# Reordering a hybrid decoder block: preparation, branch loads and the seam before the feed-forward part

## The chip, the cores and the metric

The kernel runs on one core of one Trainium2 chip. What counts is the time of one execution on the device in microseconds (us), the median of several. An execution that is profiled has a time and a span (first to last instruction) of its own.

## The reference: what is computed

One layer of a decoder trunk in float32, 1024 tokens of width 1024:

```python
h = rms_norm(x, norm1_g); proj = h @ w_in                      # 1024 x 6912
p_rwkv, p_sb, q_mem, gate_logits = split(proj)
y_a = rwkv7_branch(p_rwkv, ...)       # 8 heads of 64: token shift, decay, delta-rule recurrence
y_b = stick_breaking_branch(p_sb, q_g, k_g)      # 8 heads of 64, causal, q and k normed
y_m = memory_branch(q_mem, mem, ...)  # 4 heads of 128 over 256 memory tokens
x = x + (sum_b sigmoid(gate_b) * (y_b @ w_branch[b])) @ w_out
h = rms_norm(x, norm2_g) @ w_up                                # 1024 x 5632
acc = causal_conv3(h); gate, val = split(acc)
x = x + (silu(gate) * val) @ w_down
```

## The kernel before

Products that need float32 accuracy are made of three passes of the fast type fp32r: a matrix is split in a rounded high part (ScalarE, ACT: a copy, L80) and a low part (a subtraction on GpSimd, POOL, L81, or on VectorE, DVE), and `mm3` adds hi*hi, hi*lo and lo*hi for two 128x512 halves in PSUM. Eight k steps of this make one 128x1024 tile of a projection: 48 matmuls on TensorE (PE).

The program runs in these stages. `startup` (L171) loads x transposed in eight tiles and three weight tiles, splits them (`xhi`, `xlo`), and makes the squares for the norm. `rwkv_prep` (L307) prepares the recurrence for four pairs of heads: `shift_item` projects k, r and v and passes them to `shifted` (L242), which multiplies by the row norm (L248), makes the shifted copy on ACT (L249) and combines both on DVE (L251); `chain` (L374) makes `bk` (L381) and `ra` (L382 to L384), `gram` (L388) has PE multiply them and DVE mask the result (L398), `decayed` and `turned` make what PE transposes. Then follow stick-breaking attention (`sb_attn`, L814), memory attention (`mem_attn`, L1029, with `mem_q` at L1006), the recurrence by chunks (`inverse`, `stage2`, L477), group norm, and the branch products. `branch` (L1145) loads a stored branch output (`load_y`, L1106, DMA at L1110), splits it (`split_y`, L1101 on ACT, L1102 on DVE) and multiplies it by w_branch.

The projections are *items*: generators that yield after every k step. `weave` runs a stage as the main line and takes items from the list in `run` (L1698) as filler, so that PE has a projection between the steps of a stage; `gate_item` (L733) is such a filler, and its `hook` runs a function after a given k. `close_gates` (L710) does the sigmoids of finished gates. The framework's scheduler fixes the order of each engine when the program is built; instructions that are `pinned` keep the order of the program text among themselves, others may be moved. Every engine then runs its list strictly in order, SyncE (SP) its list of DMA issues too.

After these, `out_proj` (L1200) multiplies by w_out for eight token tiles, and `norm` (L1222) and `spread` (L1238) bring each tile normed and transposed into the operand of the up projection. That projection uses a 2x2 scheme with seven products of half size: `sums` (L1257) makes sums of quarters of the operand, called T1 to T4 beside the quarters 11, 21 and 22, and `split` (L1268) makes the high (L1271, ACT) and low part (L1272) of each. `up_phase` (L1326) runs `step(n, i)` for the products i of pair n; the beginning of this part, where the last tile is normed while the first products run, is called the seam. `weight_sums` and the `prep` functions make the weights' sums and splits (L1351, L1354). `down_phase` is untouched.

The tiles come from pools of a fixed number of buffers: three of tag `w4`, four of `A`, eight of `qk`, seven of `at`. A tile's first writer waits until the readers of the buffer's last tile are done; for a load this wait is in SP's list.

## Time and profile before

| | before |
|---|---|
| median of 3 runs | 1858.47 us (1855.64 to 1860.42) |
| profiled execution: its time | 1856.43 us |
| its span | 1854.7 us |
| PE busy in it | 1796.9 us (97%) |
| DVE, ACT, POOL busy | 1170.1, 866.7, 788.6 us |
| mean granted TensorE clock | 0.991 |
| read from and written to device memory | 179 MB, 80 MB |

A line of waits reads: engine and its line, what it waited for, us in total, times, the longest. A line of the timeline reads: start, duration, engine, line, operation, output and inputs, and in brackets how long the engine stood idle before it and for what. A line of windows reads: the stretch, its length, busy time and count of PE, PE's weight loads, DVE, ACT and POOL, then the granted clock, the DMA share and GB/s. All matmuls are issued by the helpers at L112 and L105, so tiles tell them apart: `mm` banks hold projections, `g` banks everything small.

### The profile page before, as it was taken

Reading aid. Unit: us, or ns where it says so; the run is one execution under the profiler, and the core shown is the slowest. Engines: PE = TensorE matmul, PEld = TensorE weight load, DVE = VectorE, ACT = ScalarE, POOL = GpSimd, SP = SyncE. Lnnn points to the kernel's source line nnn. Section 1 sums busy time; section 2 is a strip of 40 time slices with the busy share of each in tenths; the row PEclk is TensorE's granted clock in tenths of the full one; section 3 lists DMA queues with packets and bytes.
Section 4 is the critical chain, followed back from the end, with each engine's and each line's share of the span. In section 5 each row is a group of like instructions: output and inputs, shape, how many; then the busy total and the mean of one; then the engine's idle time right before and its main releaser. Section 6 shows DMA issues by size and latency. Waiting matters only on the chain. (4 is left out here: it accounts for less than half of the span.)

```text
span 1854.7 us, 27269 instructions
## 1 busy us (share of the span) xinstructions
PE 1796.9 (97%) x10468; PEld 1451.4 (78%) x10468; DVE 1170.1 (63%) x1623; ACT 866.7 (47%) x1553; POOL 788.6 (43%) x447
## 2 busy tenths in 40 slices
PE   8999999999999999998999999979999999999999
PEld 6777778778787887776777878768888888878877
DVE  5657664998887514334333882467776777785595
ACT  5443343565565635533443443454454444444433
POOL 2322343222221452122322541487776767545454
PEclk9999999999999999999999999999999999999999
DMA  4155465111112441568654462323232233395475
GB/s 180 58 170 182 158 201 187 49 43 64 40 52 78 112 128 40 177 237 281 229 171 161 163 235 102 114 68 109 95 124 88 97 114 108 120 326 203 141 247 185
DMA packets 122339, 261.28 MB, mean 141 GB/s; under 512 B 28505, under 2 KB 43097, under 8 KB 122082
## 3 DMA queue, kind: packets, MB, share of 16 engines
q1 hardware_dynamic: 84738, 193.71, 32.2%
q10 hardware_dynamic: 33696, 53.23, 7.9%
q0 software_dynamic: 3776, 12.62, 2.2%
q8 instruction: 82, 1.34, 0.3%
q14 instruction: 47, 0.39, 0.1%
HBM read 178.99 MB, written 80.48 MB: 140 GB/s over the span
## 5 line engine op out<-in xcount | busy, mean ns | idle before, releaser
L81 POOL TENSOR_TENSOR wl<-wr,wh 128x1024 fp32r<-128x1024 f32 x77 | 195.0, 2533 | 479.8 <-ACT wh L80 479.8
L112 PE MATMUL mm<-xhi,wh 128*128 128x512 f32 x784 | 266.0, 420 | 9.1 <-ACT xhi L182 7.4
L112 PE MATMUL mm<-xlo,wh 128*128 128x512 f32 x784 | 247.2, 397 | 0.7 <-DVE xlo L183 0.7
L112 PE MATMUL mm<-xhi,wl 128*128 128x512 f32 x784 | 244.4, 393 | 0.0
L112 PEld LDWEIGHTS mm<-xlo,wh 128*128 128x128 f32 x784 | 149.5, 191 | 35.1 <-DVE xlo L183 1.5
L112 PEld LDWEIGHTS mm<-xhi,wl 128*128 128x128 f32 x784 | 148.9, 190 | 33.8 <-POOL wl L81 0.5
L112 PEld LDWEIGHTS mm<-xhi,wh 128*128 128x128 f32 x784 | 138.5, 192 | 39.8 <-issue 9.1
L80 ACT ACTIVATE wh<-wr 128x1024 fp32r<-128x1024 f32 x77 | 81.5, 1059 | 153.8 <-PE mm L112 89.6
L112 PE MATMUL mm<-dw,da 128*128 128x512 f32 x528 | 121.3, 390 | 1.5 <-DVE da L1593 1.4
L112 PE MATMUL mm<-BT,l 128*128 128x512 f32 x504 | 117.9, 389 | 1.0 <-POOL l L1354 1.0
L112 PEld LDWEIGHTS mm<-dw,da 128*128 128x128 f32 x528 | 98.9, 188 | 23.3 <-DVE da L1593 2.3
L1594 POOL TENSOR_TENSOR dw<-draw,dw 128x512 fp32r<-128x512 f32 x55 | 80.5, 1471 | 84.9 <-ACT dw L1592 82.2
L112 PE MATMUL mm<-BT,wh 128*128 128x512 f32 x352 | 109.8, 393 | 3.2 <-DVE u L1406 3.2
L838 DVE TENSOR_TENSOR_SCAN at<-at,nrt 128x128 f32<-128x128 f32 (+3 forms) x64 | 91.2, 1428 | 32.3 <-ACT at L832 32.2
L112 PEld LDWEIGHTS mm<-BT,l 128*128 128x128 f32 x504 | 94.5, 188 | 21.0 <-POOL l L1354 1.4
L112 PE MATMUL mm<-B,wh 128*128 128x512 f32 x352 | 108.5, 389 | 2.1 <-ACT p L1448 2.1
L1593 DVE TENSOR_TENSOR da<-draw,da 128x512 fp32r<-128x512 f32 x77 | 67.0, 878 | 60.3 <-ACT da L1591 59.7
L112 PE MATMUL g<-dw,da 128*128 128x512 f32 x396 | 92.4, 394 | 2.2 <-ACT dw L1592 1.1
L1354 POOL TENSOR_TENSOR l<-it,l 128x1024 fp32r<-128x1024 f32 x21 | 50.8, 2421 | 94.4 <-ACT l L1351 94.4
L112 PEld LDWEIGHTS g<-dw,da 128*128 128x128 f32 x396 | 75.4, 191 | 18.7 <-ACT dw L1592 1.6
L1591 ACT ACTIVATE da<-draw 128x512 fp32r<-128x512 f32 x77 | 48.3, 629 | 84.3 <-PE mm L112 41.0
L169 POOL TENSOR_TENSOR hf<-rs,half 128x16 f32<-128x16 f32 (+1 forms) x17 | 48.5, 2856 | 86.1 <-DVE rs L168 85.7
(329 smaller groups left out, 3982.2 us busy)
## 6 DMA issues: line engine op xcount, KB each, us to landing
wr<-in_w_in_dram SPq DMA_DIRECT2D x50, 512.0 KB, 3.6
draw<-actd SPq DMA_DIRECT2D x77, 256.0 KB, 3.4
draw<-in_w_down_dram SPq DMA_DIRECT2D x55, 256.0 KB, 4.6
at<-scr SPq DMA_DIRECT2D x24, 512.0 KB, 6.2
wr<-in_w_up_dram SPq DMA_DIRECT2D x22, 512.0 KB, 3.5
actd<-gall ACTq DMA_DIRECT2D x44, 256.0 KB, 3.3
rw<-in_w_up_dram SPq DMA_DIRECT2D x20, 512.0 KB, 3.9
gsd<-w ACTq DMA_DIRECT2D x18, 512.0 KB, 2.7
```

What stands on the lines that cost most here:

```text
L80: self.nc.scalar.activation(hi, raw, AF.Copy)
L81: self.nc.gpsimd.tensor_tensor(lo, raw, hi.bitcast(F32), ALU.subtract)
L112: self.pinned(self.nc.tensor.matmul(*a, **k))
L169: nc.gpsimd.tensor_tensor(out, t[:, :n], self.half[:, :n], ALU.pow)
L838: self.pinned(nc.vector.tensor_tensor_scan(sn[:, :W][:, ::-1], sn[:, :W][:, ::-1], self.nrt[:, 1152 - W :][:, ::-1], 1.0, ALU.mult, ALU.max))
L1354: nc.gpsimd.tensor_tensor(lo, src, hi.bitcast(F32), ALU.subtract)
L1591: self.pinned(nc.scalar.activation(A[:, 0], a, AF.Copy))
L1593: self.pinned(nc.vector.tensor_tensor(A[:, 1], a, A[:, 0].bitcast(F32), ALU.subtract))
L1594: nc.gpsimd.tensor_tensor(Wt[:, 1], w, Wt[:, 0].bitcast(F32), ALU.subtract)
```

## The change

At the start the first weight and x tile come in two halves each, with splits of halves; the squares follow one tile late; the parameters' load stands behind the first half of the weight; and eight bf16 matmuls on a tile of zeros stand in front, into a bank that nobody reads. `shifted` returns its last step as a function, which `shift_item` calls one yield later. `chain` makes `ra` ahead of `bk`. `norm_quarter` yields three times ahead of its scaling, and `close_gates` runs at k = 4. In `mem_kv` the sums for the two halves of the memory norm are two items, and in `mem_q` the split is pinned. Branch loads go into `A` tiles, in whose place the low part is then written, and are split in hooks 3 to 6 of the gate item behind the load. At the seam, `norm` is a generator, the low and high splits are separate functions whose order is written out, p's copy is separate from its product, and the splits of 11 and 21 come at tiles 3 and 4.

```diff
+        halves = [slice(0, 512), slice(512, 1024)]
+        idle = self.t4("ys", BF16, 512)
+        nc.vector.memset(idle, 0.0)
+        pt = self.ps("g")
+        for _ in range(8):
+            nc.tensor.matmul(pt, idle[:, :128], idle, start=True, stop=True)
...
+        def square(k):
             sq = self.t4("qk")
-            nc.scalar.activation(sq, raw, AF.Square)
+            nc.scalar.activation(sq, raws[k], AF.Square)
...
+            parts = halves if k == 0 else [slice(0, 1024)]
+            if k == 0:
+                raww = self.pool_wt.tile([128, 1024], F32, name=self.nm("wr"), tag="wr", bufs=2)
+                ws.append(weights(0))
+                for hs in halves:
+                    nc.sync.dma_start(raww[:, hs], self.I["w_in"][first[0]][:, hs])
+                    if hs.start == 0:
+                        nc.sync.dma_start(self.params, self.I["params"])
+                    nc.sync.dma_start(raw[:, hs], src[:, hs])
+                self.split_raw(raww[:, halves[0]], *[w[:, halves[0]] for w in ws[0]])
+            else:
+                if k < 6 and k % 2 == 0:
+                    raww = self.load_w(self.I["w_in"][first[k // 2]])
+                nc.sync.dma_start(raw, src)
+            for hs in parts:
+                nc.scalar.activation(hi[:, hs], raw[:, hs], AF.Copy, scale=self.par("g1", k))
+                nc.vector.scalar_tensor_tensor(lo[:, hs], raw[:, hs], self.par("g1", k), hi[:, hs].bitcast(F32), ALU.mult, ALU.subtract)
+            if k == 0:
+                self.split_raw(raww[:, halves[1]], *[w[:, halves[1]] for w in ws[0]])
+            elif k < 6 and k % 2 == 0:
+                ws.append(self.split_raw(raww, *weights(k)))
+            if k:
+                square(k - 1)
+        square(7)
...
-        out = self.t4(tag)
-        nc.vector.scalar_tensor_tensor(out, pr, self.omm[:, ti : ti + 1], tmp, ALU.mult, ALU.add)
-        return out
+
+        def rest():
+            out = self.t4(tag)
+            nc.vector.scalar_tensor_tensor(out, pr, self.omm[:, ti : ti + 1], tmp, ALU.mult, ALU.add)
+            return out
+
+        return rest
...
-        out.append(self.shifted(ti, "at", pp))
+        rest = self.shifted(ti, "at", pp)
+        yield
+        out.append(rest())
         self.fresh.append(name)
-        yield
...
             bk4, ra4 = (x.rearrange("p (c u s) -> p c u s", c=8, u=2) for x in (bk, ra))
+            nc.vector.tensor_tensor(ra4[:, :, 0], self.c8(r[:, hs]), self.c8(P[:, hs]), ALU.mult)
+            nc.vector.scalar_tensor_tensor(ra4[:, :, 1, 1:64], self.c8(P[:, hs])[:, :, 0:63], -1.0, self.c8(kk[:, hs])[:, :, 1:64], ALU.mult, ALU.mult)
+            nc.vector.tensor_scalar(ra4[:, :, 1, 0], self.c8(kk[:, hs])[:, :, 0], -math.exp(OFF), None, ALU.mult)
             for x, first in ((b, 1), (kp, 0)):
                 for h2 in range(2):
                     q = slice(h2 * 64, h2 * 64 + 64)
                     nc.vector.tensor_tensor(bk4[q, :, first ^ h2], self.c8(x[q, hs]), self.c8(Q[q, hs]), ALU.mult)
-            nc.vector.tensor_tensor(ra4[:, :, 0], self.c8(r[:, hs]), self.c8(P[:, hs]), ALU.mult)
-            nc.vector.scalar_tensor_tensor(ra4[:, :, 1, 1:64], self.c8(P[:, hs])[:, :, 0:63], -1.0, self.c8(kk[:, hs])[:, :, 1:64], ALU.mult, ALU.mult)
-            nc.vector.tensor_scalar(ra4[:, :, 1, 0], self.c8(kk[:, hs])[:, :, 0], -math.exp(OFF), None, ALU.mult)
             self.spill(p, h, 0, ra, nc.sync)
...
-        for _ in range(2):
+        for _ in range(3):
             yield
         turned(0, bp)
         bp = decayed(1, u1[0])
-        for _ in range(4):
+        for _ in range(3):
             yield
...
         self.rsqrt(rs, vs, 16, 1.0 / 64, 64e-5)
-        yield
+        for _ in range(3):
+            yield
...
-            if k == 2:
+            if k == 4:
...
-                nc.scalar.activation(qhi[:, hs], pp[i], AF.Copy, scale=self.par("memq"))
+                self.pinned(nc.scalar.activation(qhi[:, hs], pp[i], AF.Copy, scale=self.par("memq")))
                 nc.scalar.activation(sq[:, hs], pp[i], AF.Square)
-                nc.vector.scalar_tensor_tensor(qlo[:, hs], pp[i], self.par("memq"), qhi[:, hs].bitcast(F32), ALU.mult, ALU.subtract)
+                self.pinned(nc.vector.scalar_tensor_tensor(qlo[:, hs], pp[i], self.par("memq"), qhi[:, hs].bitcast(F32), ALU.mult, ALU.subtract))
...
-        ys = []
+        hi = self.pool_a.tile([128, 4, 1024], F32R, name=self.nm("yhi"), tag="inst")
+        los = [self.t4("A", F32R) for _ in range(4)]
         for k in range(4):
-            y = self.t4("w4")
-            self.nc.sync.dma_start(y, self.yd[b, k])
-            ys.append(y)
-        return self.split_y(ys)
+            self.nc.sync.dma_start(los[k].bitcast(F32), self.yd[b, k])
+
+        def part(k):
+            y = los[k].bitcast(F32)
+            self.pinned(self.nc.scalar.activation(hi[:, k], y, AF.Copy))
+            self.pinned(self.nc.vector.tensor_tensor(los[k], y, hi[:, k].bitcast(F32), ALU.subtract))
+
+        return [(hi[:, k], los[k]) for k in range(4)], [lambda k=k: part(k) for k in range(4)]
...
-            st["y"] = self.load_y(b)
+            st["y"], parts = self.load_y(b)
+            hooks.update({3 + k: parts[k] for k in range(4)})
...
-            x = self.t4()
+            x = self.t4() if tt < 7 else l4("x7", F32)
             sq = self.t4() if tt < 7 else self.pool_l.tile([128, 1024], F32, name="sq7", tag="sp", bufs=1)
             nc.sync.dma_start(x, self.I["x"][tt * 128 : (tt + 1) * 128, :])
...
+            yield
+            self.pinned(nc.vector.tensor_tensor(rs, ss[:, 0:1], ss[:, 1:2], ALU.add))
             self.rsqrt(rs, rs, 1, 1.0 / D, 1e-6)
+            yield
+            self.pinned(nc.scalar.activation(sq, x, AF.Copy, scale=rs))
...
         def late(tt):
             spread(tt, sqs.pop(tt))
             if tt == 3:
-                for i in (0, 1):
-                    operand(("11", "21")[i], self.pool_l, "l4")
-                    split(("11", "21")[i], [halves(j)[i] for j in range(2)], nc.gpsimd)
+                side(0)
...
+        def evacuate(n):
+            p1 = st[n, "p1"] = self.r4("p1", n=512)
+            ins = nc.scalar.activation(p1, st[n, "A"], AF.Copy)
+            if n < 2:
+                self.pinned(ins)
+
         def step(n, i):
             if i == 1:
                 A = st[n, "A"] = bank()
                 product(n, 1, A, True, True)
-                p1 = st[n, "p1"] = self.r4("p1", n=512)
-                nc.scalar.activation(p1, A, AF.Copy)
+                if n:
+                    evacuate(n)
             elif i == 2:
...
         prep1(1)
-        split("T2", src["T2"], nc.vector, old)
-        split("22", src["22"], nc.gpsimd, old)
+        hi("22", old)
+        hi("T1", old, (0,))
+        hi("T2", old)
+        next(norm)
+        lo("T1", old, (0,))
+        next(norm)
+        hi("T1", old, (1,))
+        lo("T2", old)
+        lo("22", old, eng=nc.gpsimd)
         step(0, 1)
-        step(1, 1)
-        late(7)
-        split("T2", src["T2"], nc.vector, new)
-        split("22", src["22"], nc.gpsimd, new)
+        evacuate(0)
+        next(norm, None)
+        st[1, "A"] = bank()
+        product(1, 1, st[1, "A"], True, True)
+        spread()
+        evacuate(1)
+        sums(384, 512, (0,))
+        hi("T1", new)
+        lo("T1", new, (0,))
+        lo("T1", js=(1,))
+        hi("T2", new)
+        lo("T2", new)
         load(1)
-        prep2(0)
-        parts("T1", nc.vector)
         step(0, 2)
+        hi("T3", old)
         step(1, 2)
         prep3(0)
-        parts("T3", nc.vector)
+        sums(384, 512, (1,))
+        lo("T3", old)
+        hi("T3", new)
+        lo("T3", new)
+        hi("22", new)
+        lo("22", new, eng=nc.gpsimd)
         operand("T4", self.pool_a, "A", bufs=4)
-        split("T4", src["T4"], nc.vector)
+        hi("T4")
+        lo("T4")
+        prep2(0)
         st[0, 3] = hl(self.early[3][:, R], self.pool_l, ("l4", "l4"), 512, True)
-        for i in (6, 5, 7, 4, 3):
-            step(0, i)
-            if i == 5:
-                prep2(1)
-            if i == 4:
-                load(2)
+        step(0, 5)
+        prep2(1)
+        step(0, 6)
+        Bk = bank()
+        product(0, 7, Bk, True, True)
+        v = st[0, "u2"] = u_tile()
+        nc.vector.tensor_tensor(v[:, L2], Bk, st[0, "u1"][:, R2], ALU.add)
+        nc.vector.tensor_tensor(v[:, R2], st[0, "C"], v[:, L2], ALU.add)
+        step(0, 40)
+        step(0, 41)
+        load(2)
+        step(0, 3)
         prep3(1)
         for n in range(1, len(pairs)):
             order = (6, 5, 40, 7, 41, 3) if n == 1 else (1, 5, 6, 2, 7, 4, 3)
...
-            items += [*([self.differ] if p == 0 else []), kp, gate(), *([self.spread_last] if p == 0 else []), kss, qp, gate(hooks), mark(f"sb{p}")]
+            items += [*([self.differ] if p == 0 else []), kp, gate({6: self.spread_last} if p == 0 else {}), kss, qp, gate(hooks), mark(f"sb{p}")]
...
-        ld1, br1 = self.branch(1, True)
-        ld2, br2 = self.branch(2, False)
-        items += [lambda: drain(inv), ld1, gate(), gate(), mark("y1"), *br1, ld2, gate(), *br2, gate()]
+        ld1, hk1, br1 = self.branch(1, True)
+        ld2, hk2, br2 = self.branch(2, False)
+        items += [lambda: drain(inv), gate(), ld1, gate(hk1), mark("y1"), *br1, ld2, gate(hk2), *br2, gate()]
```

Three places show what this does to the engines' lists. First DVE in the preparation of the first pair (`g` to `at` at L398, in the change L435, is a mask; L251, in the change L285, the last step of a token shift; L381 to L384 and L415 to L421 belong to `chain`). Before:

```order
L382 TENSOR_TENSOR qk_807<-at_518,qk_495 128x8x64
L383 SCALAR_TENSOR_TENSOR qk_807<-qk_495,at_426 128x8x63
L384 TENSOR_SCALAR qk_807<-at_426 128x8
L248 TENSOR_TENSOR w_97_718<-mm_625,nrt 128x512
L246 MEMSET w_120_851 128x1
L251 SCALAR_TENSOR_TENSOR at_724<-w_97_718,omm,w_98_719 128x1024
L398 TENSOR_TENSOR at_768<-g_769,kon 128x4x128
L398 TENSOR_TENSOR at_768<-g_770,kon 128x4x128
L398 TENSOR_TENSOR at_790<-g_791,kon 128x4x128
L398 TENSOR_TENSOR at_790<-g_792,kon 128x4x128
```

and with the change:

```order
L415 TENSOR_TENSOR qk_824<-at_536,qk_512 128x8x64
L469 SCALAR_TENSOR_TENSOR at_633<-at_633,params,qk_579 128x1024
L416 SCALAR_TENSOR_TENSOR qk_824<-qk_512,at_443 128x8x63
L417 TENSOR_SCALAR qk_824<-at_443 128x8
L285 SCALAR_TENSOR_TENSOR at_751<-w_99_735,omm,w_100_736 128x1024
L421 TENSOR_TENSOR qk_823<-qk_498,qk_499 64x8x64
L435 TENSOR_TENSOR at_785<-g_786,kon 128x4x128
L435 TENSOR_TENSOR at_785<-g_787,kon 128x4x128
L421 TENSOR_TENSOR qk_823<-qk_498,qk_499 64x8x64
L421 TENSOR_TENSOR qk_823<-qk_514,qk_499 64x8x64 x2
L435 TENSOR_TENSOR at_807<-g_808,kon 128x4x128
L435 TENSOR_TENSOR at_807<-g_809,kon 128x4x128
```

The token shift's last step stood straight ahead of the four masks, behind the second half of its product (L248); now both halves of that product stand further ahead, other work lies between, and the masks come in two pairs with `chain` products between and behind the step.

Second, ACT where the second branch is loaded (L1101, in the change L1155, is the split of y; L549 and L586 are the same copy in the recurrence). Before:

```order
L80 ACTIVATE wh_7571<-wr_7569 128x1024
L1101 ACTIVATE yhi_7556<-w_1310_7548 128x1024
L549 ACTIVATE qk_7234<-g_7469 64x64 x2
L549 ACTIVATE qk_7234<-g_7470 64x64
L1101 ACTIVATE yhi_7556<-w_1311_7550 128x1024
L549 ACTIVATE qk_7234<-g_7470 64x64
L549 ACTIVATE qk_7239<-g_7471 64x64 x2
L549 ACTIVATE qk_7239<-g_7472 64x64 x2
```

and with the change:

```order
L80 ACTIVATE wh_7572<-wr_7570 128x1024
L586 ACTIVATE qk_7247<-g_7482 64x64 x2
L586 ACTIVATE qk_7247<-g_7483 64x64 x2
L586 ACTIVATE qk_7252<-g_7484 64x64 x2
L586 ACTIVATE qk_7252<-g_7485 64x64 x2
L1155 ACTIVATE yhi_7561<-A_7562 128x1024
L1155 ACTIVATE yhi_7561<-A_7563 128x1024
```

The four copies for the recurrence were mixed with the two splits; now they stand ahead of them. In SP's list the four loads of y, which stood in three places among the recurrence's loads, now stand together. (In memory attention, on DVE, two `nb` of L1050 that stood behind the two L1017 of the third query stand ahead of them in the change, and on ACT four exponentials of L1053 stand ahead of that query's L1015 and L1016.)

Third, POOL at the seam (L1272, in the change L1326, is the low split of an operand; L169 and L168 are the last multiplication of a norm's `ss`). Before:

```order
L169 TENSOR_TENSOR ss_1608_10174<-rs_10181,half 128x1
L1272 TENSOR_TENSOR B_1_0_10237<-raw_9862,B_0_0_10235 128x1024
L1272 TENSOR_TENSOR B_1_1_10238<-raw_9862,B_0_1_10236 128x1024
L1272 TENSOR_TENSOR B_1_0_10245<-raw_9862,B_0_0_10243 128x1024
L1272 TENSOR_TENSOR B_1_1_10246<-raw_9862,B_0_1_10244 128x1024
L169 TENSOR_TENSOR ss_1616_10272<-rs_10279,half 128x1
L1303 TENSOR_TENSOR wsum_10352<-wsec_10351 128x512
```

and with the change:

```order
L168 TENSOR_TENSOR ss_1602_10183<-rs_10190,half 128x1
L1326 TENSOR_TENSOR B_1_0_10246<-raw_9871,B_0_0_10244 128x1024
L1326 TENSOR_TENSOR B_1_1_10247<-raw_9871,B_0_1_10245 128x1024
L168 TENSOR_TENSOR ss_1610_10273<-rs_10280,half 128x1
L1326 TENSOR_TENSOR B_1_0_10286<-raw_9871,B_0_0_10284 128x1024
L1326 TENSOR_TENSOR B_1_1_10287<-raw_9871,B_0_1_10285 128x1024
L1361 TENSOR_TENSOR wsum_10361<-wsec_10360 128x512
```

One `ss` has moved from behind the four splits to between the second and the third.

139 lines of the change are left out of this document (75 added, 64 removed).

## The prediction

> **What bounds the kernel now.** I read the page's busy times and chain first, then TensorE's waits, then its granted clock around the longest waits, and last the timeline of the engine that each wait names. The first two:
>
> ```profile
> PE 1796.9 (97%) x10468; PEld 1451.4 (78%) x10468; DVE 1170.1 (63%) x1623; ACT 866.7 (47%) x1553; POOL 788.6 (43%) x447
> ...
> PE 30%; DVE 1%; issue 1%; POOL 1%; ACT 0%; POOLq 0%; DVEq 0%
> ```
>
> TensorE (PE) is busy for 1796.9 of 1854.7 us, and of what the chain names nearly all is its matmuls. So only two things can be won: the 57.8 us in which PE does nothing, and matmuls that run at a lower clock. The waits of PE that the change can touch:
>
> ```profile
> PE mm L112 <- ACT xhi L182: 7.4, 1, 7.4
> PE g L105 <- DVE at L398: 6.4, 3, 2.6
> PE g L112 <- ACT qk L549: 6.0, 1, 6.0
> PE g L105 <- ACT at L850: 3.7, 2, 2.8
> PE mm L112 <- DVE u L1406: 3.2, 2, 2.5
> PE g L112 <- ACT at L1053: 2.8, 1, 2.8
> PE g L112 <- DVE qk L384: 2.3, 2, 1.7
> PE mm L112 <- ACT p L1448: 2.1, 1, 2.1
> PE g L105 <- ACT w L1235: 2.1, 1, 2.1
> ...
> PE g L105 <- DVE at L838: 1.6, 1, 1.6
> ...
> PE mm L112 <- POOL l L1354: 1.0, 1, 1.0
> PE mm L112 <- POOL wl L1354: 0.9, 1, 0.9
> ...
> PE mm L112 <- DVE BT L1272: 0.6, 1, 0.6
> ```
>
> (Columns: us in total, times, the longest.) Most are two or three microseconds, once or a few times: an instruction that stands a few places too late in an engine's order. Each can cost a second time. These windows start at such a wait; the column behind POOL is PE's clock:
>
> ```profile
> 100.00:110.00 10.00, 7.77 (x32) 6.33 (x31) 5.36 (x11) 4.56 (x5) 3.55 (x2) 0.83 0.67 238
> 151.00:161.00 10.00, 8.32 (x52) 6.21 (x51) 9.91 (x14) 2.21 (x2) 2.37 (x1) 0.83 0.77 275
> 493.00:503.00 10.00, 7.22 (x37) 5.68 (x37) 9.45 (x11) 3.30 (x6) 0.00 (x0) 0.83 0.30 105
> 715.00:725.00 10.00, 7.23 (x58) 5.99 (x58) 4.56 (x14) 6.82 (x21) 2.35 (x2) 0.83 0.25 67
> 867.00:880.00 13.00, 6.96 (x58) 5.55 (x56) 8.45 (x13) 5.16 (x16) 2.72 (x2) 0.74 0.88 308
> 1168.00:1178.00 10.00, 7.92 (x32) 6.22 (x31) 1.60 (x5) 2.93 (x6) 5.49 (x5) 0.83 0.38 107
> 1223.00:1233.00 10.00, 7.82 (x26) 5.98 (x27) 2.78 (x6) 3.01 (x4) 9.92 (x7) 0.83 0.09 18
> ```
>
> A clock of 0.83 over 10 us is 1.7 us of full-speed time lost; 0.74 over 13 us is 3.4. What a slow stretch does to the matmuls is seen at the start, where the clock first rises:
>
> ```profile
> 12.05 1.05 PE L112 MATMUL mm<-xlo,wh 128*128 128x512 f32 x2
> 12.90 1.05 PE L112 MATMUL mm<-xhi,wh 128*128 128x512 f32 x2
> ...
> 15.62 0.62 PE L112 MATMUL mm<-xhi,wh 128*128 128x512 f32 x2
> 16.08 0.62 PE L112 MATMUL mm<-xlo,wh 128*128 128x512 f32 x2
> ```
>
> Two matmuls every 0.85 us before, every 0.46 us after: 0.43 against 0.23 us each. So a 2-us wait is worth nearly 4 where the clock falls behind it.
>
> [...]
>
> **The start (A).** Weight and x now come in halves, so ACT can make the first half of wh and xhi about 2 us sooner. But PE is not limited by its first matmul there:
>
> ```profile
> 17.38 3.44 POOL L81 TENSOR_TENSOR w<-wr,w 128x1024 fp32r<-128x1024 f32 x1 [3.39 <-ACT w L80]
> ```
>
> This is the low part of the third weight, ready at 20.8 us; PE had caught up with it by then, and POOL had stood 3.39 us for ACT's high part. In the new order that high part stands ahead of the fifth xhi and the squares come one tile later, so it moves up by 1 to 1.5 us; against that the extra half instructions add about 1 us to ACT. The eight small matmuls in front have no row. Bounds: 8 times 0.23 to 0.43 is 1.8 to 3.4 us, beside the first loads, for which PE stands 7.4 us anyway, so hidden either way; cover gone, they would cost up to 1 us. If they leave the clock up, the matmuls before 15.6 us are faster, but these wait for data. I take -0.3, between -2 (the split 1.5 us sooner and the last cold matmuls warm) and +1.2.
>
> [...]
>
> **Preparation, 50 to 350 us (B).** DVE runs its order as it stands, and a late ACT result holds everything behind it:
>
> ```profile
> 101.48 1.28 DVE L251 SCALAR_TENSOR_TENSOR at<-w,omm,w 128x1024 f32<-128x1024 f32 x1 [1.21 <-ACT w L249]
> 102.69 2.48 DVE L398 TENSOR_TENSOR at<-g,kon 128x512 f32<-128x512 f32 x4
> ```
>
> The last step of the token shift (L251) waits 1.21 us for ACT and runs 1.28, with four gram masks (L398) behind it, for which PE stands (6.4 us in three waits). The change puts that step into `rest()` behind a yield, so one work item later, with the third yield before `turned` and the product for `ra` ahead of the others. The work is the same and nothing is added. The masks then stand behind other DVE work of 0.6 to 2 us instead of a wait. I count all of L398 (-6.4), half of L384's longest (-0.8) and two dips (-3.4); later `decayed` work on POOL and a DVE that is still full at 151 us (9.91 of 10) give back 1.1. B = -9.5, bounds -13 and -4.
>
> **Stick-breaking attention, 300 to 620 us (C).** Here DVE is nearly as full as PE:
>
> ```profile
> 450.00:500.00 50.00, 46.31 (x306) 37.88 (x305) 46.40 (x42) 30.03 (x53) 15.08 (x7) 0.97 0.18 59
> ```
>
> `spread_last` moves into the sixth hook of a gate item, `close_gates` from the third to the fifth k, and the scale behind `norm_quarter` two yields later. The wait for L838 (1.6) should go. The one of 2.8 us at 493 us (L850) has the same DVE work ahead of it, so it stays, its dip too. With 46.4 of 50 us taken, a place won on DVE is a place lost to another: -2, bounds -6 and +2.
>
> **Memory attention (D).**
>
> ```profile
> 715.22 0.75 DVE L1017 SCALAR_TENSOR_TENSOR qk<-mm,params,qk 128x512 fp32r<-128x512 f32 x1 [3.02 <-ACT w L1016]
> ...
> 716.95 0.22 DVE L1050 SCALAR_TENSOR_TENSOR nb<-mxt,hf 128x2 f32<-128x2 f32 x2
> ```
>
> The tiny nb (L1050) that the exponentials need stands behind two L1017 that wait 3.02 us for ACT. In the new order both nb, and on ACT the exponentials, stand ahead of that query's last steps. The two L1017 come later, into a gap of DVE, and their reader is the next head. -2.8 and one dip of 1.7: D = -4.5, bounds -4.5 and -1.
>
> **Branch loads (E).** The longest wait, 6.0 us at 867:
>
> ```profile
> 871.73 1.06 ACT L1101 ACTIVATE yhi<-w 128x1024 fp32r<-128x1024 f32 x1 [4.83 <-DMA w<-yd]
> 872.81 1.17 ACT L549 ACTIVATE qk<-g 64x64 f32<-64x64 f32 x5
> ...
> 868.27 0.33 SPq L1110 DMA_DIRECT2D w<-yd  x1
> ```
>
> The y load got its buffer only at 868.27, ACT stood 4.83 us for it at L1101, and PE needs the L549 behind it. In the change the loads go into four A tiles and their splits into hooks 3 to 6 of the gate item that follows. On ACT the four L549 now stand ahead of the split. So the 6.0 us and both cold stretches (3.4) go: -9.4. Kept as risk: the A tiles come free when the branch before is done, and SP's queue stands still until then, with loads of the recurrence's next step behind. Before, those stood behind the y load of 868.27, so there is some slack. Lower bound of the gain -2.
>
> **The seam, 1160 to 1250 us (F).** PE waits in turn for six things (L1235, L1448, L1406, BT, and l and wl of L1354). Two of the causes:
>
> ```profile
> 1159.73 9.47 POOL L1272 TENSOR_TENSOR B<-raw,B 128x1024 fp32r<-128x1024 f32 x4 [6.38 <-ACT B L1271]
> ...
> 1216.02 9.84 POOL L1354 TENSOR_TENSOR wl<-wsec,wh 128x1024 fp32r<-128x1024 f32 x1 [2.09 <-ACT wh L1351]
> ```
>
> Four low splits of 2.37 us each stand on POOL ahead of the norm's tiny ss, for which ACT's L1235 waits. The change does two, then ss, then two. Later the hi splits on ACT and the lo splits on DVE are ordered by first use, and p's evacuation stands ahead of them. Added: one tile (x7), nothing in work. Removed: 2.1 + 2.1 + 2.5 + 1.0 + 0.9 + 0.6 = 9.2 us and two dips, 3.4. Since the same ACT and DVE work must be done before PE's third product, I give back 0.6 for the last spread: F = -12, bounds -14 and -5.
>
> **Sum.** -0.3 - 9.5 - 2 - 4.5 - 9.4 - 12 = -37.7. The down phase is unchanged. PE, when it comes sooner at one place, meets the next producer with less lead. The listed waits of 0.6 to 1.6 us show how thin such leads are, so I add four new ones of 1 us: +4. Profiled time 1856.4 - 33.7 = 1822.7; the median of the runs shown (1858.47) lies 2.0 above the profiled time, hence 1824.7, taken as **1824 us**. From the bounds of the parts, not all at one end: 1814 to 1834.
>
> **Rivals.**
> 1. *The waits move.* DVE at 46.4 of 50 us and ACT's unbroken row at the seam hand back half: B -4, C 0, D -2, E -7, F -6, and 2 elsewhere = -17 or so: 1841. For it: the DVE rows above; against it: E and D are single places with idle engines around them.
> 2. *Nearly every gap goes.* All waits quoted (40.1 us in sum) but 6 us of the first, that is 34.1, with the dips counted above (11.9) and the one at 493 us (1.7), nothing handed back: 1858.5 - 47.7 = 1811. For it: each has one late producer with idle time elsewhere; against it: the wait at 493 us is untouched.
> 3. *The dips stay.* If the clock falls because windows are filled with small matmuls and not because of the wait, only waits are won: 1824 + 8.5 to 11.9, so 1834. Against it: each window above begins at a wait.
> 4. *SP's queue stands (slower).* SP issues in order, and a load can hold it long:
>
> ```profile
> 700.15 16.79 SPq L76 DMA_DIRECT2D wr<-in_w_in_dram  x2
> ```
>
> Two issues held it 16.8 us here. If the y loads of each branch wait as long for an A tile, the recurrence's loads behind them starve: twice 16.8, two further cold stretches (3.4 each) and E's 9.4 not won: 1824 + 50 = 1874. It makes the kernel slower from 12 us for each branch (1864 - 1824 - 16.2, halved). Against it: the wait at 867 us itself shows branch 1's products to be done by then.
> 5. *It does nothing.* The order in the text is set, yet the late things are data: only a part of D and E comes, within 5 us of before: 1854.
>
> **Chances.** Forecast 0.52, waits move 0.20, nearly all 0.10, dips stay 0.06, nothing 0.06, slower 0.06. Range 1811 to 1845: it takes in rival 2's floor and rival 1 with its scatter, and leaves out 4 and 5. A measurement tells 0.3% (5.6 us) from no change: faster 0.86 (the first four, less 0.02 of rival 1), same 0.08, slower 0.06.
>
> **What would show it.** Right: TensorE's busy time near 1785 (the dips), its waits of 2 us and more reduced to the start, the 493-us one and at most two others, a clock of 1.0 in the windows of 100, 715 and 867 us, and on POOL ss between the B splits. Wrong: a wait of PE for a split of y (the new L1155) or of the recurrence's loads; waits for gram masks that are back at the next pair; a seam whose waits are as long in sum, under other names. A first matmul at 5 us with PE's next stop at 20 would bear out that A is worth nothing.

## The result and the profile after

| | before | changed |
|---|---|---|
| median | 1858.26 us (4 runs, 1855.64 to 1860.42) | 1836.67 us (4 runs, 1835.09 to 1838.31) |
| ratio | 1 | 0.9884, 95% interval 0.9867 to 0.9902 |
| profiled execution: time, span | 1856.43, 1854.7 us | 1838.31, 1836.5 us |
| PE busy, share of the span | 1796.9 us, 97% | 1793.6 us, 98% |
| span less PE busy | 57.8 us | 42.9 us |

The change made the kernel 21.6 us faster, 1.16%; the forecast was 34. The busy line of the page:

```profile
PE 1793.6 (98%) x10476; PEld 1446.1 (79%) x10476; DVE 1172.7 (64%) x1624; ACT 867.1 (47%) x1555; POOL 785.6 (43%) x448
```

The eight small matmuls at the start are in PE's busy time with 3.6 us, so PE's own work shrank by 6.9 us (3.3 + 3.6) and the time without work by 11.3 (14.9 - 3.6). Together these are the 18.2 us of the spans. The same line of the trace, PE's waits, shows what is left:

```profile
PE mm L112 <- POOL wl L81: 4.6, 3, 2.3
PE g L105 <- ACT at L888: 4.3, 2, 3.8
...
PE g L112 <- ACT qk L598: 2.2, 2, 1.4
PE g L105 <- DVE at L876: 2.1, 1, 2.1
...
PE g L112 <- DVE qk L421: 2.1, 2, 1.1
PE g L105 <- DVE at L435: 2.1, 1, 2.1
PE mm L112 <- DVE u L1538: 1.6, 1, 1.6
...
PE mm L112 <- POOL l L1416: 1.6, 1, 1.6
```

In the changed kernel L435 is the gram mask (L398 before), L421 is `bk` (L381), L888 the attention's output copy (L850), L876 the scan (L838), L598 the recurrence's copy (L561) and L1416 the weights' low split of the up projection (L1354). The waits for the branch load (6.0), for p (2.1), for the norm's w (2.1) and for memory attention's exponentials (2.8) are gone. The masks are down from 6.4 to 2.1. But the low part of a weight, which cost nothing before, now costs 4.6, and two waits of the attention have grown (3.7 to 4.3, 1.6 to 2.1). Granted clock, in windows at the same work as those of the prediction (column behind POOL):

```profile
98.00:108.00 10.00, 10.00 (x59) 8.10 (x56) 8.70 (x15) 3.71 (x5) 4.11 (x2) 1.00 0.87 311
211.00:221.00 10.00, 7.94 (x36) 6.07 (x36) 4.97 (x7) 3.56 (x5) 2.84 (x2) 0.83 0.54 184
259.00:269.00 10.00, 7.66 (x48) 5.64 (x47) 9.96 (x9) 1.86 (x2) 5.83 (x2) 0.83 0.63 217
492.00:502.00 10.00, 6.18 (x24) 4.83 (x23) 9.66 (x11) 3.26 (x6) 0.00 (x0) 0.83 0.29 105
713.00:723.00 10.00, 10.00 (x82) 8.40 (x81) 5.53 (x17) 7.71 (x20) 3.16 (x2) 1.00 0.25 67
864.00:877.00 13.00, 11.78 (x127) 9.01 (x127) 8.45 (x16) 6.02 (x21) 3.20 (x3) 1.00 1.01 379
1158.00:1168.00 10.00, 10.00 (x50) 8.38 (x49) 2.42 (x6) 4.23 (x9) 9.35 (x7) 1.00 0.32 107
```

The lower clock is gone from 98, 713, 864 and 1158 us, and it is new at 211 and 259 us, where waits are now.

PE's list has the same length in both kernels but for the eight small matmuls, so the two traces can be laid side by side: I take the start of the matmul with the same number in PE's order.

| up to matmul | before, us | changed, us | difference | change in this part (minus: won) | forecast |
|---|---|---|---|---|---|
| 300 (start, A) | 69.06 | 69.53 | +0.5 | +0.5 | -0.3 |
| 750 | 158.09 | 152.70 | -5.4 | -5.9 | |
| 1750 (end of preparation, B) | 330.15 | 329.08 | -1.1 | +4.3; B in all -1.5 | -9.5 |
| 3750 (stick-breaking, C) | 632.40 | 632.76 | +0.4 | +1.4 | -2 |
| 4500 (memory, D) | 747.26 | 744.73 | -2.5 | -2.9 | -4.5 |
| 5500 (branch load, E) | 887.92 | 878.56 | -9.4 | -6.8 | -9.4 |
| 7250 | 1103.02 | 1095.58 | -7.4 | +1.9 | 0 |
| 8000 (seam, F) | 1283.92 | 1266.68 | -17.2 | -9.8 | -12 |
| 10250 (down phase) | 1796.71 | 1779.42 | -17.3 | 0 | 0 |

The last microsecond to the 18.2 of the spans lies in the tail. The 1.9 us lost between matmuls 5500 and 7250 went in pieces of 0.2 to 0.8 us around 970 and 1078 us; a second execution of the changed kernel, shown below, lost 0.9 in this part. The cause is open. (The forecast also had +4 for new waits without a place.) Most of what is missing is in one part: the preparation won 5.9 us by matmul 750 and gave 4.3 back.

The places that came as forecast look like this. POOL at the seam, with ss now between the splits (L168 is the norm's ss, L1326 the low split):

```profile
1152.32 4.79 POOL L1326 TENSOR_TENSOR B<-raw,B 128x1024 fp32r<-128x1024 f32 x2 [6.38 <-ACT B L1321]
1157.46 0.55 POOL L168 TENSOR_TENSOR ss<-rs,half 128x1 f32<-128x1 f32 x1 [0.35 <-DVE rs L167]
1157.97 4.74 POOL L1326 TENSOR_TENSOR B<-raw,B 128x1024 fp32r<-128x1024 f32 x2
```

And the branch load, SP's issue and ACT's split:

```profile
857.15 4.76 SPq L1151 DMA_DIRECT2D A<-yd  x4
...
865.93 2.09 ACT L1155 ACTIVATE yhi<-A 128x1024 fp32r<-128x1024 f32 x2 [1.33 <-DMA A<-yd]
```

SP does stand for the A tiles, 4.76 us for four loads, and ACT waits 1.33 us for the first of them. Nothing that PE needs soon is behind either.

### The profile page after: what moved, and what is told of

Same layout as the page of the kernel before. It is cut to its first block, busy times and chain, and to the rows that moved or that the text cites. A ratio compares the mean times of both kernels' runs of the same rounds, so it can differ in the third digit from the quotient of the medians.

```text
span 1836.5 us, 27309 instructions
## 1 busy us (share of the span) xinstructions
PE 1793.6 (98%) x10476; PEld 1446.1 (79%) x10476; DVE 1172.7 (64%) x1624; ACT 867.1 (47%) x1555; POOL 785.6 (43%) x448
## 4 chain that ended last, share of the span: by engine, by line
PE 66%; DVE 7%; issue 4%; POOL 2%; DMA 2%; ACT 2%; SPq 0%; ACTq 0%; POOLq 0%; DVEq 0%
PE mm L112 54%; PE g L112 10%; PE g L105 2%; DVE it L501 1%; POOL dw L1687 1%; DVE at L876 1%; DVE mg L1245 1%; DVE inst L503 1%; DVE qk L839 1%; DMA wr<-in_w_out_dram 1%; DVE qk L822 1%; POOL wl L81 0%; DVE qk L823 0%; DMA qk<-vd 0%; DVE at L1237 0%
## 5 line engine op out<-in xcount | busy, mean ns | idle before, releaser
L81 POOL TENSOR_TENSOR wl<-wr,wh 128x1024 fp32r<-128x1024 f32 (+1 forms) x78 | 195.6, 2509 | 511.3 <-ACT wh L80 503.0
L80 ACT ACTIVATE wh<-wr 128x1024 fp32r<-128x1024 f32 (+1 forms) x78 | 81.7, 1048 | 156.7 <-PE mm L112 97.6
L112 PEld LDWEIGHTS mm<-BT,l 128*128 128x128 f32 x504 | 94.5, 188 | 21.6 <-POOL l L1416 2.0
L876 DVE TENSOR_TENSOR_SCAN at<-at,nrt 128x128 f32<-128x128 f32 (+3 forms) x64 | 87.5, 1371 | 34.3 <-ACT at L870 34.0
L1416 POOL TENSOR_TENSOR l<-it,l 128x1024 fp32r<-128x1024 f32 x21 | 50.8, 2417 | 92.1 <-ACT l L1413 92.1
L778 DVE TENSOR_TENSOR w<-w,nrt 128x1024 f32<-128x1024 f32 x24 | 50.0, 2085 | 58.4 <-ACT w L777 58.4
```

What stands on the lines that cost most here:

```text
L80: self.nc.scalar.activation(hi, raw, AF.Copy)
L81: self.nc.gpsimd.tensor_tensor(lo, raw, hi.bitcast(F32), ALU.subtract)
L112: self.pinned(self.nc.tensor.matmul(*a, **k))
L778: nc.vector.tensor_tensor(g, g, self.nrb, ALU.mult)
L876: self.pinned(nc.vector.tensor_tensor_scan(sn[:, :W][:, ::-1], sn[:, :W][:, ::-1], self.nrt[:, 1152 - W :][:, ::-1], 1.0, ALU.mult, ALU.max))
L1416: nc.gpsimd.tensor_tensor(lo, src, hi.bitcast(F32), ALU.subtract)
```

## The experiments

**Each large part alone, in the kernel before.** Edits: `prep_only` takes the changed `shifted`, `shift_item` and `rwkv_prep`; `branch_only` the changed `load_y`, `branch` and the three lines on them in `run`; `seam_only` the changed `out_proj` and `up_phase`.

> The kernel before with the preparation's edits alone (the last step of the token shift one yield later, ra ahead of bk, three yields ahead of the first turn). Theory 1 (the gain of the first pairs is handed back at the third and fourth pair by the edits themselves): 1 to 2 us faster, the waits for gram masks at 101 and 151 us gone, a wait for masks near 212 us and one for a weight's low part near 260 us there. Theory 2 (the gain is real and is lost in the changed kernel to its other parts): 6 to 10 us faster. By my forecast for this part alone: 9.5 us faster.

> The kernel before with the branch loads' edits alone (y into A tiles, splits in hooks 3 to 6, the gate item ahead of the first load). Theory 1: 6.8 us faster, all at 867 to 880 us, the two windows of lower clock gone. By my forecast 9.4. Theory 2 (SyncE's queue hands it back): a new wait of the recurrence's loads and under 5 us.

> The kernel before with the seam's edits alone (norm as a generator, high and low splits apart and ordered by first use, splits of 11 and 21 at tiles 3 and 4). Theory 1 (the parts add, being far apart in time): 9.8 us faster, as the two traces differ between 1160 and 1284 us. Theory 2 (part of that difference came from PE's earlier arrival): under 7 us.

| kernel | median, us | before it, us | ratio, 95% interval |
|---|---|---|---|
| prep_only | 1853.03 | 1857.10 | 0.9977 (0.9960 to 0.9995) |
| branch_only | 1852.36 | 1857.53 | 0.9982 (0.9968 to 0.9995) |
| seam_only | 1847.89 | 1857.53 | 0.9951 (0.9936 to 0.9966) |

The preparation alone is 4 us faster, between the two theories' numbers, and PE's waits in it are those of the changed kernel (there L403 is the mask, L389 `bk`):

```profile
PE mm L112 <- POOL wl L81: 2.7, 1, 2.7
...
PE g L112 <- DVE qk L389: 2.1, 2, 1.1
PE g L105 <- DVE at L403: 2.1, 1, 2.1
```

In the trace it is 6.0 us ahead at matmul 750, 3.5 at 1750 (3.4 of it behind the start) and 2.8 at 3750. So it is the preparation's own edits that hand the gain back, not the other parts. The branch loads win 6.8 us between matmuls 5250 and 5500, as in the changed kernel, though only 3.3 us (0.18%) in the ratio; no wait for the recurrence's loads came. The seam wins 8.4 us in its stretch of the trace and 9.1 by the ratio; what is left of its waits are these:

```profile
PE g L105 <- ACT sq L1237: 1.6, 1, 1.6
PE mm L112 <- DVE u L1491: 1.6, 1, 1.6
PE mm L112 <- POOL l L1369: 1.6, 1, 1.6
```

The parts add up roughly: 4.3 + 3.3 + 9.1 = 16.7 by the ratios, and the memory part comes on top.

**Why the preparation hands back: the order of bk and ra.**

```diff
-            (three instructions for ra4)
             for x, first in ((b, 1), (kp, 0)):
                 ... bk4 ...
+            (three instructions for ra4)
```

> The changed kernel with bk ahead of ra again. Theory 1 (GpSimd's decayed waits for the last bk, and the weight's low split stands behind it): the wait for the low part near 259 us (2.3 us) goes with its dip (1.7), the waits for bk near 148 and 203 us (1.1 and 1.0) go too or turn into waits for ra of 0.5 to 1.7 us; 2 to 4 us faster than the changed kernel. Theory 2 (PE, being earlier, meets the weights' loads): the wait near 259 us stays over 2 us, time within 1 us.

In the changed kernel POOL at this place reads (L447 is `decayed`, L81 the weight's low split):

```profile
256.88 1.90 POOL L447 TENSOR_TENSOR it<-qk,pc 128x1024 f32<-128x1024 f32 x1 [9.02 <-DVE qk L421]
258.74 6.09 POOL L81 TENSOR_TENSOR wl<-wr,wh 128x1024 fp32r<-128x1024 f32 x2
```

POOL stood 9.02 us for the last bk, with a split behind it whose high part was made at 252.2 to 253.3 us. With bk first:

```profile
253.79 2.34 POOL L447 TENSOR_TENSOR it<-qk,pc 128x1024 f32<-128x1024 f32 x1 [6.12 <-DVE qk L418]
256.09 2.84 POOL L81 TENSOR_TENSOR wl<-wr,wh 128x1024 fp32r<-128x1024 f32 x1
...
256.00:266.00 10.00, 10.00 (x65) 7.58 (x64) 9.89 (x11) 2.10 (x2) 4.78 (x3) 1.00 0.61 197
```

The last line is the window from 256 to 266 us: PE is busy throughout, at full clock. The wait of 2.3 us is gone with its lower clock, so theory 1 is borne out as to the wait. Others came: 0.9 us for masks at 104 us, 1.7 for bk at 150 with the lower clock behind it, and 1.2 for masks at 268. The wait for masks at 212 us fell to 0.3, but not because the masks are made sooner: the step of the token shift still stands directly ahead of all four, and it is PE that comes later to this place. From matmul 300 to 1750 the trace takes 3.4 us less than the changed kernel's first execution and 1.7 less than its second.

Median 1833.96 us, ratio to before 0.9868 (0.9838 to 0.9898), 2.7 us under the changed kernel's median. The two intervals overlap, and the profiled execution took 1838.85 us, no less than the changed kernel's, with a wait of 3.1 us at the seam's last tile. The gain in time is likely, but not clear of noise.

**Why the preparation hands back: the token shift's last step.**

```diff
         rest = self.shifted(ti, "at", pp)
         yield
-        out.append(rest())
+        self.rests.append(lambda: out.append(rest()))
...
+            if k == 2:
+                self.late_rests()
```

> The changed kernel with the last step of the token shift run at k = 2 of the next projection item instead of one yield after its own; in the list of VectorE two of the four masks near 212 us then stand ahead of it. Theory 1 (the order of these two decides): the wait for masks near 212 us falls from 2.1 to under 1 us and the lower clock at 214 us goes, 2.5 to 3.5 us faster than the changed kernel. Theory 2 (VectorE's work ahead of the masks decides, not the step): the wait stays over 1.5 us, time within 1 us.

VectorE in the changed kernel, third pair:

```profile
211.75 1.28 DVE L285 SCALAR_TENSOR_TENSOR at<-w,omm,w 128x1024 f32<-128x1024 f32 x1 [1.21 <-ACT w L281]
212.96 2.48 DVE L435 TENSOR_TENSOR at<-g,kon 128x512 f32<-128x512 f32 x4
```

That is the picture of 101 us before: the step waits 1.21 us for ACT, with four masks behind it. With the step at k = 2 (there L443 is the mask and L286 the step):

```profile
207.80 1.29 DVE L443 TENSOR_TENSOR at<-g,kon 128x512 f32<-128x512 f32 x2
...
212.32 2.71 DVE L286 SCALAR_TENSOR_TENSOR at<-w,omm,w 128x1024 f32<-128x1024 f32 x1 [1.21 <-ACT w L282]
```

Two masks now run at 207.8 us. The wait at 212 us is gone, and the one at 148 us as well; the one at 255 us (2.3) stays, being the other cause. In the trace 3.7 us are won between matmuls 1000 and 1250 against the changed kernel's first execution, and 2.1, the wait alone, against its second, which had no lower clock there. Median 1834.07 us, ratio to before 0.9872 (0.9848 to 0.9897); the interval overlaps with that of the changed kernel, whose eight executions took 1835.09 us or more, these four 1835.22 or less.

**The eight small matmuls.**

```diff
-        idle = self.t4("ys", BF16, 512)
-        nc.vector.memset(idle, 0.0)
-        pt = self.ps("g")
-        for _ in range(8):
-            nc.tensor.matmul(pt, idle[:, :128], idle, start=True, stop=True)
```

> The changed kernel without the eight small matmuls on zeros. Theory 1 (the start is bound by the third weight's low part at 20.6 us): PE's progress at 30 us within 0.3 us of the changed kernel, time the same within 1 us, the clock rises near 13 to 15 us. Theory 2 (the matmuls bring the clock up earlier): the clock rises one 3.4-us window later and 1 to 2 us are lost.

1837.35 us, ratio 0.9890 (0.9864 to 0.9916), the same as with them. The clock rises at 12.2 us without them, at 13.0 with them, and at matmul 250 the kernel with them is 0.4 us ahead; between the nine traces whose start is the same code this number differs by up to 1.35 us. In five of the nine the clock does come up behind them, at 4.2 to 5.2 us, and is lost again at 7.6 to 8.6 while PE waits for data. So it is in `rest_k2` (columns as above):

```profile
4.00:8.00 4.00, 1.29 (x3) 0.19 (x1) 1.39 (x5) 1.43 (x3) 1.26 (x1) 1.00 0.92 295
8.00:12.00 4.00, 3.13 (x7) 2.10 (x7) 2.30 (x2) 3.99 (x6) 1.28 (x1) 0.51 1.03 416
```

**The attention: two candidates for its longer waits.**

```diff
-            if k == 4:
+            if k == 2:
                 self.close_gates()
```

> The changed kernel with close_gates at k = 2 again. Theory 1 (the later sigmoid and the step of the inverse that now stands ahead of its factor on VectorE make ScalarE stand 6.0 us instead of 5.0 at 488 us): the wait near 492 us falls from 3.8 to 2.8 us, 1 us faster than the changed kernel. Theory 2 (the step ahead is there because spread_last and the gate item moved): the wait stays at 3.8 and the time the same within 1 us.

```diff
-kp, gate({6: self.spread_last} if p == 0 else {}), kss, qp, gate(hooks)
+kp, gate(), *([self.spread_last] if p == 0 else []), kss, qp, gate(hooks)
```

> The changed kernel with spread_last as an item of its own again, as before. Theory 1 (the item it no longer is shifted every later step of the inverse by one against the main work, so that at 492 us one more step stands ahead of the gate's factor and at 343 us ahead of the scan): the wait near 492 us falls from 3.8 to 2.8 us, the one near 343 us from 2.1 to 1.6; 1.5 us less waiting, time 1 to 2 us faster than the changed kernel. Theory 2 (VectorE's total work there decides): both stay, time the same within 1 us.

The first changes nothing: 1836.29 us, and the wait for L888 stays at 3.8. The second does: the waits for L888 and L876 are back at 2.8 and 1.6, and the trace wins 1.8 us between matmuls 1750 and 3750. Its median is 1834.85 us, ratio 0.9890 (0.9872 to 0.9908), beside 1837.24 and 0.9902 (0.9886 to 0.9919) for the changed kernel in the same series, which alone would not show it. In the changed kernel VectorE and ScalarE read:

```profile
492.35 1.12 DVE L503 TENSOR_TENSOR inst<-inst,it 128x920 f32<-128x920 f32 x1
493.38 1.22 DVE L778 TENSOR_TENSOR w<-w,nrt 128x1024 f32<-128x1024 f32 x1
...
494.64 1.06 ACT L781 ACTIVATE w<-w 128x1024 f32<-128x1024 f32 x1 [6.03 <-DVE w L778]
```

and with spread_last as an item:

```profile
489.89 1.23 DVE L778 TENSOR_TENSOR w<-w,nrt 128x1024 f32<-128x1024 f32 x1
...
491.15 1.06 ACT L781 ACTIVATE w<-w 128x1024 f32<-128x1024 f32 x1 [4.99 <-DVE w L778]
```

The inverse (L501, L503) is paced by counting items. One item fewer puts every later step of it one place further on against the main work, and at this place a step of 1.1 us lands ahead of the gate's factor for which ScalarE stands.

**Memory attention: the split sums, and the pinned query.**

```diff
-lambda: mss(0), mv[0], lambda: mss(1), *mv[1:]
+lambda: (mss(0), mss(1)), *mv
```

> The changed kernel with both sums of the memory norm in one item again. Theory 1 (the split item put the weight's high split on ScalarE behind the attention's output copies, which wait for PE): the wait for a low part near 658 us (1.4 us) goes, 1 to 1.5 us faster than the changed kernel. Theory 2 (it comes from the attention's own order): stays, no difference.

```diff
-                self.pinned(nc.scalar.activation(qhi[:, hs], pp[i], AF.Copy, scale=self.par("memq")))
+                nc.scalar.activation(qhi[:, hs], pp[i], AF.Copy, scale=self.par("memq"))
...
-                self.pinned(nc.vector.scalar_tensor_tensor(qlo[:, hs], pp[i], ...))
+                nc.vector.scalar_tensor_tensor(qlo[:, hs], pp[i], ...)
```

> The changed kernel with the query's split (qhi on ScalarE, qlo on VectorE) not pinned; in the list of VectorE the third head's two nb then stand behind that query's two low parts again. Theory 1 (that order is the whole cause of the 2.8 us): a wait of PE for the exponentials of 2.5 to 3 us is back near 714 us, 3 to 4 us slower than the changed kernel in the trace, 1839 to 1841 us. Theory 2 (the earlier weight split or the shifted queue of items had removed it): no such wait, the same time within 1 us.

With the sums joined, the wait for the low part at 658 us is gone (1.6 us won at that place), but a window of lower clock came at 627 us and took 1.3; the time, 1837.93 us, shows no gain.

That window belongs to the edit. One sum is 32 matmuls of one column, and joined they are 64 in a row:

```profile
623.81 2.03 PE L112 MATMUL g<-kon,w 128*64 128x1 f32 x64
```

Of the six traces with the sums joined, five (`prep_only`, `branch_only`, `seam_only`, this one and `best2` below) have a window of lower clock right behind these 64, and the kernel before has none. Of the eight with the sums apart none has one there. PE did not wait: in the 10 us ahead of each window no gap of PE is over 0.03 us. In `best2`, the stretch with the 64 and the window behind it:

```profile
615.60:619.10 3.50, 3.50 (x76) 2.89 (x75) 1.88 (x3) 2.03 (x3) 0.76 (x1) 0.99 0.00 0
619.10:622.50 3.40, 3.40 (x13) 2.71 (x11) 2.79 (x3) 1.89 (x3) 3.40 (x3) 0.50 0.00 0
```

So the split of the sums brought a wait, and kept a window of lower clock away that cost about as much; neither the prediction nor the expectation speaks of the window.

Without the pins the wait is back (L1094 is the exponential), with 3.2 us lost in this stretch of the trace. The median is 1839.43 us, 2.8 above the changed kernel's; the ratio, 0.9899 (0.9868 to 0.9929), can't tell the two apart, so it is the trace that shows it:

```profile
PE g L112 <- ACT at L1094: 2.8, 1, 2.8
```

**The changed kernel once more.**

> The changed kernel once more, nothing edited. Theory 1 (whether a wait of 1 to 3 us brings the lower clock depends on where it falls in the clock's own 3.4-us windows): the same waits of PE at the same places within 0.2 us, but other windows of lower clock than at 214, 262, 498 and 979 us, one or two of them gone or new. Theory 2 (each such wait brings it): the same waits and the same four windows.

1837.24 us, ratio 0.9902 (0.9886 to 0.9919), and in the profiled execution a span of 1833.5 us instead of 1836.5. The waits agree within 0.2 us from 47 to 1240 us. Three of the four windows of lower clock stand behind the same waits again; the one at 214 us is gone, one near the end is new, and so is one of 6.8 us at the start. This execution's window with the wait for masks, and the one near the end:

```profile
209.00:219.00 10.00, 7.94 (x38) 5.99 (x36) 6.45 (x11) 3.50 (x5) 2.41 (x2) 1.00 0.40 136
...
1776.00:1786.00 10.00, 7.82 (x27) 5.76 (x26) 8.22 (x10) 4.61 (x8) 6.06 (x4) 0.83 0.71 224
```

and the latter in the first execution of the same program:

```profile
1776.00:1786.00 10.00, 7.94 (x34) 6.02 (x33) 9.81 (x13) 2.94 (x5) 3.63 (x3) 1.00 0.71 216
```

The same wait of 2.1 us at 212 us brought the lower clock in one execution and not in the other.

**Together.** The changed kernel with `bk_first`, `rest_k2`, `mss_joint` and `spread_item`:

> The changed kernel with four edits together: bk ahead of ra again, the last step of the token shift at k = 2 of the next item, both sums of the memory norm in one item, spread_last an item of its own. If they add: the waits at 148, 212, 259, 658 us gone or under 1 us, those at 343 and 492 at 1.6 and 2.8; some 8 us less waiting than the changed kernel and 1 to 3 windows of lower clock fewer, 1824 to 1830 us. If bk ahead of ra and the later step get in each other's way on VectorE: 1830 to 1834 us.

1831.29 us (1827.75 to 1832.38), ratio to before 0.9866 (0.9849 to 0.9882), and 6 us under the changed kernel in the same series, whose interval (0.9886 to 0.9919) lies above this one. PE's waits (L896 is the output copy, L443 the mask, L1292 the norm's scaling of the last tile):

```profile
PE g L106 <- ACT at L896: 3.7, 2, 2.8
...
PE g L106 <- DVE at L443: 2.5, 3, 1.2
...
PE g L106 <- ACT sq L1292: 1.8, 1, 1.8
```

The waits at 212, 259 and 658 us are gone and the one at 492 is back at 2.8, as expected, and 6.6 us are won up to matmul 10250. The wait for bk at 148 us stayed (1.1). The scan's wait near 343 us, expected at 1.6, is not there at all.

The median lies in the range of the second theory, 1830 to 1834 us. Three shorter waits for masks are there (0.9, 1.2 and 0.5 us; the first two came with bk first alone too), and one of 1.8 us at the seam's last tile. That one was 0.2 us in the changed kernel and between 0.2 and 3.1 in other traces with the same seam; its cause is open. And two windows of lower clock, at 305 and 619 us, came with two of the edits: the 64 matmuls of the joined sums, and at 305 us another 64 small ones in a row, which the changed kernel, with no item for `spread_last`, runs as 32 and 32.

## Why the prediction came out as it did

The direction, the bound by PE and the places of the large waits were right; the size was forecast at 34 us and is 21.6. Step by step:

- **Start (A), -0.3.** Right that it is worth nothing: PE's first matmul on data came at 5.8 instead of 7.4 us and its stop for the third low part at 20.7, as before. The 0.5 us lost up to matmul 300 are within the 1.35 us by which traces with this start differ. The clock's rise behind the small matmuls, and its loss again while PE waited for data, was seen in five of nine traces (0.51 from 8 to 12 us in `rest_k2`).
- **Preparation (B), -9.5, measured -1.5** (-3.2 in the changed kernel's second execution, -3.4 in `prep_only`; neither has the lower clock at 214 us). This is the step that failed. "I count all of L398 (-6.4)": I read VectorE's list for the first pair, where the step moved away from the masks, and took the others to be alike. In the third pair's list the step stands directly ahead of all four masks, as before, and the wait is 2.1 us there. The prediction had named this among its signs of being wrong: masks that are waited for again at a later pair. And "later decayed work on POOL ... give back 1.1" was the right mechanism, mis-sized: with bk last, POOL stood 9.0 us for it, with a weight's split behind it, and PE waited 2.3 us and lost clock (0.83 over the 10 us from 259 us). The two runs that undo these take their wait out. Each has a median 2.6 to 2.7 us lower, which alone is not clear of noise; the four edits together are.
- **Stick-breaking (C), -2, measured +1.4.** The scan's wait did not go; I had looked at what the edit of `spread_last` does in its own place and not at the count of items that paces the inverse. The 2.8 us at 493 us, which I had said would stay, grew to 3.8 by this.
- **Memory (D), -4.5, measured -2.9.** 4.1 us at the place named, less 1.2 lost ahead of it to the sums' split into two items, of which the prediction said nothing. That the pins are the cause was tried and holds.
- **Branch loads (E), -9.4, measured -6.8.** 5.3 of the 6.0 us of waiting went (0.8 stays, for L598). The 3.4 us for the two windows of lower clock was too much: of the 6.83 us won in this part 5.25 are the wait, so 1.6 us is what the windows cost. Of their 6.8 us PE waited for 1.6 and then ran small matmuls for 3.3. SP's queue stood 4.8 us and hurt nobody; rival 4 is out, `branch_only` shows no loss.
- **Seam (F), -12, measured -9.8** (8.4 alone). The waits for w, p and u went. In the place of L1354's 1.9 us stand 1.6 for l and 0.4, and BT still costs 0.9: the first use decides the order now, but the same work of VectorE and POOL comes before it.
- **Lower clock.** 11.9 us were counted from seven windows (1.7 for each of the five in B, D and F, together the 8.5 of rival 3, and 3.4 for the two in E). Behind the start, ten windows became four, in both executions but not the same four, and PE's own work fell by 6.9 us, so rival 3 (the dips stay) did not come. But its reason was not empty, and "each window above begins at a wait" holds only for the windows picked there: seven windows in five other traces begin behind 64 small matmuls in a row, without a wait. And the same wait does not bring the lower clock each time (the 2.1 us at 212 us did in one of two executions of the changed kernel), so a single trace counts it too high or too low.
- **New waits, +4.** Of the right size, and they have places: 259 us, 658 us, and the growth at 343 and 492 us come to 5.3 us. By the number, rival 3 (1834) lies nearest to 1836.7 and rival 1 (1841) next. By what happened, rival 1 (the waits move) comes closest, though not for its reason: the order of lists, not the fullness of VectorE, handed the time back, since each of four edits in the order took its wait out again. What `bk_first` and `best2` show beside it is that such an edit also brings smaller waits at other places.

## What to carry to other kernels

When an edit works by moving instructions in an engine's list, read the list at every place where the pattern comes again, not at the first; the scheduler put the same step back in front of the masks two pairs later. Anything that counts items, yields or slots to pace other work moves that work everywhere behind the edit. And where a kernel's clock falls in places, judge a 2-us edit by the wait itself in the trace and by several executions: two of the same program differed by 3.0 us here. An edit that lines up very small matmuls is worth a look at the clock too: here seven of twelve rows of 64 had a lower clock behind them without any wait.

## What was not expected of the hardware

Windows of half clock are 3.4, 6.8 or 10.2 us long in all traces here, but where the end of the program cuts one, and whether a given wait brings one differs between executions of the same work. The 2.1 us at 212 us did once and did not in the repeat. `prep_only` and the kernel before run the same program from 340 us on, with the same waits, but the 6.0-us wait for the branch load brought 6.8 us of lower clock in the kernel before and 10.2 in the other. Two executions of the changed kernel differ by 3.0 us in their spans, 2.6 of it by matmul 8000, with waits that agree within 0.2 us from 47 us to there. In the profiled execution of the kernel before, and in the first of the changed kernel, all changes of the clock lie whole multiples of 3.413 us apart. These steps do not begin with the program: the first fall is at 103.54 us in the one and at 214.34 us in the other, 110.8 us or 32.5 steps later. That the place of a wait among the steps decides whether a lower clock follows was not shown. The wait of 2.1 us at 212 us (in one execution) and that of 1.4 us at 975 us have the lower clock behind them, 0.83 over 10 us at both places.

Nor does it take a wait. Seven windows of lower clock stand behind 64 small matmuls in a row, with PE busy throughout: five behind the joined sums near 620 us (of six traces that have the 64 in a row there), and two near 305 and 310 us (of six). Where the same matmuls run as 32 and 32, with a projection's matmuls between, no trace has one (eight traces at either place). That the long row of small ones is the cause is argued from this count; the change of the sums was tried for another reason.

The other surprise is how long some instructions of VectorE took beside a split on POOL: VectorE's step L503 took 2.93 us at 341 us, while POOL ran a split of 3.10 us beside it, and 0.87 us in the kernel before, where it started with that split (341.80 and 341.81 us). There it was the scan behind it that took longer, 2.59 us beside the same split; in the changed kernel it came when the split was done, and took 0.41. An instruction on 128x8 elements shows it most plainly, in the changed kernel with POOL idle and in `bk_first` with POOL at the split that starts at 256.09 us:

```profile
252.86 0.17 DVE L417 TENSOR_SCALAR qk<-at 128x8 f32<-128x8 f32 x1
...
256.59 2.37 DVE L421 TENSOR_SCALAR qk<-at 128x8 f32<-128x8 f32 x1
```

That the two are connected is argued from the overlap alone; it was not tried.
